# A two-layer encoder: weight low halves moved to VectorE, output sums merged over two head groups, Newton steps in two operations

## The chip, the cores and the metric

The kernel runs on one core of a Trainium2 chip. The metric is the device time of one execution in microseconds (us): the median of several runs, beside one execution that was profiled. Engines are named as in the profile: PE is TensorE's matmul, PEld its weight load, DVE is VectorE, ACT is ScalarE, POOL is GpSimd, SP is SyncE, which issues most of the transfers.

## The reference

Input is a token matrix of 512 x 1024 in float32. Layer 0 mixes neighbourhood attention and a bidirectional state-space scan, layer 1 is grouped-query attention; a SwiGLU feed-forward layer follows each. The change works mostly on layer 1:

```python
def odd_mixer(x, mix_norm, w_qkv, q_norm, k_norm, w_out):
    proj = rms_norm(x, mix_norm) @ w_qkv
    q, k, v = jnp.split(proj, [1024, 1280], axis=-1)
    q = rms_norm(q.reshape(Bsz, S, 16, 64), q_norm)   # 16 query heads
    k = rms_norm(k.reshape(Bsz, S, 4, 64), k_norm)    # 4 key heads
    v = v.reshape(Bsz, S, 4, 64)
    q = apply_rope(q, cos, sin)
    k = apply_rope(k, cos, sin)
    return gqa_block_attention(q, k, v) @ w_out       # softmax over 512 keys
...
def rms_norm(x, g):
    return x * lax.rsqrt(jnp.mean(x * x, axis=-1, keepdims=True) + 1e-6) * g
...
    x = x + odd_mixer(...)
    x = x + swiglu_ffn(x, ...)
```

## The kernel before

The residual lies transposed in eight tiles `res[o]` of 128 x 512. Float32 accuracy on TensorE comes from splitting each operand: `hi` is the value rounded to the matmul's format (a copy on ScalarE), `lo` is what is left (a subtraction). `mm3` (L157) then issues three matmuls for a product: low weights by high input, high weights by low input, high by high (L160, L161, L162).

`load_w` (L139) brings a block of weights, 128 x 1024, into `raw` (two buffers), writes the high half on ScalarE (L147) and the low half with the engine given by `eng`, VectorE if none is given (L149). High and low halves have three buffers each. `stream` (L166) walks through a list of blocks, loads two blocks ahead of the one whose matmuls it yields, and yields after each step of three matmuls, so that a caller can take the matmuls piece by piece as filling between other work.

In `odd_mixer` (L1123) the order is this. `prep` (L178) splits the scaled residual, two projections into the banks `kpa` and `kpb` give the keys (`project`, L173), `sumsq` (L774) adds the squares of the residual on GpSimd (L191), and `rotate` and `head_rstd` norm and turn the keys. Query group 0 follows (`q_blocks`, L1223), then the values (L1350 to L1352), whose weights' low halves are made on GpSimd (L1341). Query groups 1 to 3, two blocks of weights each, and the output projection of head groups 0 to 2, two blocks each, are the filling of the attention loop; the low halves of all of these twelve blocks are made on GpSimd. `q_finish` (L1242) runs four steps behind the last matmul of a query group and holds the norm and the rotation, almost all on VectorE.

The attention loop has 35 steps. Step i issues scores for 256 queries of a head (`scores`: two banks, maximum on VectorE L1268, exponent on ScalarE L1270, reciprocal on VectorE L1271, scaling on GpSimd L1272), the transposes of step i - 2 (L1281, split by L1284 and L1285) and the product with the values of step i - 3 (L1298, L1299). Between them it takes so many filling steps as `quota` says:

```python
quota = (5, 5, 4) + 13 * (2,) + (3, 2, 2, 2, 2, 3, 2, 2, 2, 2, 3, 2, 2, 3, 2, 2, 3, 3, 3)
```

When a pair of heads is through, `values` splits its result into `ctxb[h // 2]` (low part on GpSimd up to head 13, L1155). `out_blocks(part)` idles, yielding nothing to do, until both pairs of its head group are there; then it multiplies for each of eight output tiles into a bank of its own and adds the bank to the residual on VectorE (L1320). Banks for this and for the query projections are three in rotation. The last head group goes through `tail` behind the loop.

An inverse square root is a logarithm and an exponent on ScalarE, improved by one Newton step in three VectorE operations: r (1.5 - 0.5 m r r). It stands in `rsqrt_tile` (L205 to L207, tiles of 128 x 512), `rsqrt_small` (L213 to L216, a few columns) and in the feed-forward layer's `norm` (L1042 to L1044).

The order of instructions on an engine is the written one only inside the feed-forward layers and, for TensorE, in the state-space part of layer 0. Elsewhere a planner orders them: in the written order, but what it takes to be ready goes ahead of what is not.

Of the kernel before, what the change touches and what calls it, by code (L numbers as in the profile page):

```python
# [12 lines left out]
ALU = mybir.AluOpType  # L13
# [4 lines left out]
P = 128  # L18
# [23 lines left out]
DT_STEP = 96  # L42
LEAD = (12, 12, 12, 0)
# [29 lines left out]
def encoder_kernel(ctx: ExitStack, tc: tile.TileContext, xt, vec, cst, rope, nab, w_v, w_qk, w_dt, w_ssd,  # L73
# [99 lines left out]
    def project(ps, src, xg, name, eng=None):  # L173
        w = load_w(src, 1024, name, eng)
        for k in range(KB):
            mm3(ps, w, k * P, xg[k], ALL, k == 0, k == KB - 1)
# [21 lines left out]

    def rsqrt_tile(m, name):
        r = slot(f"{name}_r")  # L200
        t = slot(f"{name}_t")
        A.activation(r, m, AF.Ln)
        A.activation(r, r, AF.Exp, scale=-0.5)
        A.activation(t, r, AF.Square)
        V.tensor_tensor(t, t, m, ALU.mult)  # L205
        V.tensor_scalar(t, t, -0.5, 1.5, ALU.mult, ALU.add)
        V.tensor_tensor(r, r, t, ALU.mult)  # L207
        return r

    def rsqrt_small(m, r, t):  # L210
        A.activation(r, m, AF.Ln)
        A.activation(r, r, AF.Exp, scale=-0.5)
        V.tensor_tensor(t, r, r, ALU.mult)  # L213
        V.tensor_tensor(t, t, m, ALU.mult)
        V.tensor_scalar(t, t, -0.5, 1.5, ALU.mult, ALU.add)
        V.tensor_tensor(r, r, t, ALU.mult)  # L216
# [563 lines left out]
    def ffn(layer, gname, hp):  # L780
# [232 lines left out]
        with tc.manual_schedule(engines={mybir.EngineType.PE, mybir.EngineType.DVE, mybir.EngineType.Activation}):  # L1013
# [19 lines left out]
            def norm():  # L1033
                ps = bank(f"{name}_ss", "c")
                T.matmul(ps, ones_r, ql, start=True, stop=False)
                T.matmul(ps, ones_r, qh, start=False, stop=True)
                m, r, t = (slot(f"{name}_{n}") for n in "mrt")
                A.activation(m, ps, AF.Identity, scale=1.0 / D, bias=epst)
                A.activation(r, m, AF.Ln)
                A.activation(r, r, AF.Exp, scale=-0.5)  # L1040
                A.activation(t, r, AF.Square)
                V.tensor_tensor(t, t, m, ALU.mult)  # L1042
                V.tensor_scalar(t, t, -0.5, 1.5, ALU.mult, ALU.add)
                V.tensor_tensor(r, r, t, ALU.mult)  # L1044
                rstd.append(r)
# [77 lines left out]
    def odd_mixer(op):  # L1123
# [40 lines left out]
        project(pa, w_kv[0], xg, "wka")  # L1164
        project(pb, w_kv[1], xg, "wkb")
        acc = sumsq("o")
# [56 lines left out]
        def q_blocks(g, eng):  # L1223
            banks = []

            def matmuls(w):
# [7 lines left out]
                if len(sqs) == 2:  # L1234
                    V.tensor_tensor(sqs[0], sqs[0], sqs[1], ALU.add)
                    after(4, lambda: q_finish(g, banks, sqs[0]))
# [74 lines left out]
        def out_blocks(part):  # L1311
            def matmuls(w, half):
                while ctxb[2 * part + 1] is None:
                    yield
                for o in range(4 * half, 4 * half + 4):
                    ps = bank(f"o1{part}_{o}")
                    for k in range(2):
                        mm3(ps, w, (o % 4 * 2 + k) * P, ctxb[2 * part + k], ALL, k == 0, k == 1)
                        yield
                    V.tensor_tensor(res[o], res[o], ps, ALU.add)  # L1320

            for half in range(2):
                yield (lambda half=half: load_w(w_o1[part, half], 1024, f"wo{part}_{half}", G)), \
                    (lambda w, half=half: matmuls(w, half))
# [9 lines left out]
        for c in range(4):  # L1334
# [6 lines left out]
            G.tensor_tensor(lo, part, f(hi), ALU.subtract)  # L1341
            wv.append((hi, lo))
        vhl = []
        for t in range(4):
            ps = bank(f"gv{t}", "s")
            for k in range(KB):
# [15 lines left out]
        blocks = (list(q_blocks(1, G)) + list(q_blocks(2, G)) + list(q_blocks(3, G))  # L1362
                  + [b for part in range(3) for b in out_blocks(part)])
        fill = stream(blocks, 2)
        run(fill, 8)
# [3 lines left out]
        quota = (5, 5, 4) + 13 * (2,) + (3, 2, 2, 2, 2, 3, 2, 2, 2, 2, 3, 2, 2, 3, 2, 2, 3, 3, 3)  # L1369
        lag_t, lag_v = 2, 3  # L1370
        for i in range(32 + lag_v):
            n = quota[i]
# [153 lines left out]
```

## Time and profile before

| | |
|---|---|
| median of 3 timed runs | 1289.76 us (1288.01 to 1290.24) |
| the profiled execution's own time | 1290.49 us |
| its span, first to last instruction | 1288.7 us |
| mean granted TensorE clock | 0.995 |
| busy: PE, DVE, ACT, POOL | 1264.0, 1000.4, 716.1, 166.4 us |
| the mixer of layer 1 in the span | 718 to 937 us |

Busy time is the time in which the engine's records lie; matmuls overlap in these records, so a matmul's duration is longer than its distance to the next. A wait is idle time of an engine, put down to what released it.

### The profile page before, as it was taken

How to read it: one execution, taken by the hardware profiler on the slowest of the kernel's cores; microseconds unless marked ns; L12 is line 12 of the kernel's file. 1: busy time of each engine (PE TensorE's matmuls, PEld its weight loads, DVE VectorE, ACT ScalarE, POOL GpSimd, SP SyncE). 2: the span in 40 equal slices, each digit the busy share in tenths (PEclk: the TensorE clock that was granted, in tenths of full speed). 3: DMA queues.
4: the chain of work that ended last, by engine and by line, in shares of the span. 5: the costliest groups of instructions: out<-in, count | busy, mean ns of one | idle time of the engine just before them, and what ended most of it. 6: DMA issues, size and time to landing. Idle time of an engine off the chain costs nothing.

```text
span 1288.7 us, 20006 instructions
## 1 busy us (share of the span) xinstructions
PE 1264.0 (98%) x7502; PEld 1101.0 (85%) x7502; DVE 1000.4 (78%) x1688; ACT 716.1 (56%) x1335; POOL 166.4 (13%) x184
## 2 busy tenths in 40 slices
PE   9999999989999999999999999999999999999998
PEld 8777788867888899989998778778888899889987
DVE  6788798997789898738953668998889998549732
ACT  6676568766455456514643547777565455325521
POOL 5022111011100000000002334655100000000000
PEclk9999999999999999999999999999999999999999
DMA  7334343545333333332223443321223333423132
GB/s 235 107 99 148 112 138 123 164 120 166 123 116 113 99 99 114 117 98 84 91 78 96 144 97 101 83 66 34 83 82 98 106 107 104 123 79 105 54 117 92
DMA packets 52081, 139.03 MB, mean 108 GB/s; under 512 B 6992, under 2 KB 8144, under 8 KB 51984
## 3 DMA queue, kind: packets, MB, share of 16 engines
q1 hardware_dynamic: 51696, 137.23, 34.7%
q8 instruction: 59, 0.97, 0.3%
q10 hardware_dynamic: 288, 0.52, 0.1%
q14 instruction: 38, 0.31, 0.1%
HBM read 127.11 MB, written 2.23 MB: 100 GB/s over the span
## 4 chain that ended last, share of the span: by engine, by line
PE 70%; DVE 17%; ACT 6%; issue 4%; DMA 2%; SPq 0%; POOL 0%; ACTq 0%; DVEq 0%; POOLq 0%
PE fo L160 5%; PE fo L162 5%; PE fo L161 5%; PE fa L162 5%; PE fa L161 5%; PE fa L160 5%; PE fb L161 3%; PE fb L160 3%; PE fb L162 3%; PE vps L278 2%; PE opt L1281 1%; PE fc L162 1%; PE fc L161 1%; PE fc L160 1%; PE fg L1009 1%
## 5 line engine op out<-in xcount | busy, mean ns | idle before, releaser
L147 ACT ACTIVATE wf_h<-wf_r 128x1024 fp32r<-128x1024 f32 (+1 forms) x76 | 69.5, 919 | 125.8 <-PE fo L162 68.3
L160 PE MATMUL fo<-hh,wf_l 128*128 128x512 f32 x352 | 137.2, 390 | 1.2 <-DVE wf_l L149 1.2
L161 PE MATMUL fo<-hl,wf_h 128*128 128x512 f32 x352 | 137.0, 389 | 0.0
L162 PE MATMUL fo<-hh,wf_h 128*128 128x512 f32 x352 | 136.9, 389 | 0.0
L984 DVE TENSOR_TENSOR xr<-xr,fo 128x512 f32<-128x512 f32 x48 | 32.2, 685 | 113.6 <-PE fo L162 113.6
L149 DVE TENSOR_TENSOR wf_l<-wf_r,wf_h 128x1024 fp32r<-128x1024 f32 (+1 forms) x76 | 78.8, 1053 | 15.0 <-ACT wf_h L147 15.0
L160 PEld LDWEIGHTS fo<-hh,wf_l 128*128 128x128 f32 x352 | 66.1, 188 | 15.5 <-DVE wf_l L149 2.0
L162 PEld LDWEIGHTS fo<-hh,wf_h 128*128 128x128 f32 x352 | 66.1, 188 | 13.8
L161 PEld LDWEIGHTS fo<-hl,wf_h 128*128 128x128 f32 x352 | 66.1, 188 | 13.6
L160 PE MATMUL g<-n_xh,w_l 128*128 128x512 f32 x192 | 76.6, 399 | 0.0
L162 PE MATMUL g<-n_xh,w_h 128*128 128x512 f32 x192 | 75.3, 392 | 0.0
L161 PE MATMUL g<-n_xl,w_h 128*128 128x512 f32 x192 | 75.2, 392 | 0.0
L910 ACT ACTIVATE sl<-sb 128x256 f32<-128x256 f32 x34 | 14.3, 419 | 90.7 <-DVE sb L909 90.7
L191 POOL TENSOR_TENSOR o_acc<-o_acc,o_sq 128x512 f32<-128x512 f32 x7 | 12.3, 1753 | 383.2 <-ACT o_sq L190 383.2
L1272 POOL TENSOR_SCALAR op<-op,osum 128x512 f32<-128x512 f32 x64 | 45.4, 718 | 55.5 <-DVE osum L1271 38.6
L1270 ACT ACTIVATE op<-os,omx 128x512 f32<-128x512 f32 x64 | 43.6, 686 | 15.1 <-DVE omx L1268 12.9
L1285 DVE TENSOR_TENSOR opt<-opt,opt 128x512 fp32r<-128x512 f32 x64 | 43.5, 683 | 7.2 <-ACT opt L1284 6.5
L1284 ACT ACTIVATE opt<-opt 128x512 fp32r<-128x512 f32 x64 | 37.9, 598 | 18.7 <-PE opt L1281 18.1
L791 ACT ACTIVATE sa<-fa 128x256 f32<-128x256 f32 x68 | 25.4, 374 | 36.3 <-PE fa L162 36.3
L1268 DVE TENSOR_REDUCE omx<-os 128x1 f32<-128x512 f32 x64 | 42.0, 679 | 4.5 <-PE os L1266 4.4
L791 ACT ACTIVATE gh<-gr 128x1024 fp32r<-128x1024 f32 x34 | 35.6, 1047 | 14.0 <-PE fo L162 11.6
L162 PEld LDWEIGHTS g<-n_xh,w_h 128*128 128x128 f32 x192 | 36.1, 188 | 7.5
(2644 smaller groups left out, 4363.9 us busy)
## 6 DMA issues: line engine op xcount, KB each, us to landing
ur<-in_w_fa SPq DMA_DIRECT2D x34, 512.0 KB, 3.6
gr<-in_w_fa SPq DMA_DIRECT2D x34, 512.0 KB, 3.5
w_r<-in_w_ssd SPq DMA_DIRECT2D x24, 512.0 KB, 3.7
wf_r<-in_w_fa SPq DMA_DIRECT2D x20, 512.0 KB, 3.6
wf_r<-in_w_fb SPq DMA_DIRECT2D x32, 320.0 KB, 3.0
wf_r<-in_w_fb SPq DMA_DIRECT2D x16, 512.0 KB, 3.5
wo_r<-in_w_o SPq DMA_DIRECT2D x14, 512.0 KB, 3.8
nb<-in_nab SPq DMA_DIRECT2D x16, 256.0 KB, 3.0
```

Of the source, the lines that this page charges most:

```text
L147: A.activation(hi[:, 0:cols], raw, AF.Copy)
L149: (eng or V).tensor_tensor(lo[:, 0:cols], raw, f(hi)[:, 0:cols], ALU.subtract)
L160: T.matmul(ps, wl[:, a], xh[:, b], start=first, stop=False, skip_group_check=skip)
L161: T.matmul(ps, wh[:, a], xl[:, b], start=False, stop=False, skip_group_check=skip)
L162: T.matmul(ps, wh[:, a], xh[:, b], start=False, stop=last, skip_group_check=skip)
L791: A.activation(dst, src, AF.Copy, scale=scale)
L984: V.tensor_tensor(res[o], res[o], self.banks[o], ALU.add)
L1268: V.tensor_reduce(mx, sps, AX.X, ALU.max, negate=True)
L1270: A.activation(p_, sps, AF.Exp, bias=mx, accum_out=sums)
L1272: G.tensor_scalar(p_, p_, sums, 1.0, ALU.mult, ALU.mult)
L1284: A.activation(hl[:, 0:S], pt, AF.Copy)
L1285: V.tensor_tensor(hl[:, S:2 * S], pt, f(hl[:, 0:S]), ALU.subtract)
```

## The change

- `project` loses its `eng` and gains `late`: for the first key projection the eight matmuls with the low part of the input come last. `sumsq("o")` runs on VectorE.
- The low halves of the value weights, of query groups 1 to 3 and of the output blocks are made on VectorE.
- `out_blocks` takes a list of head groups. Groups 0 and 1 form one list: each output tile is summed over both in one bank and added to the residual once, in four blocks of two output tiles; group 2 keeps two blocks of four. A block of the merged list is loaded in two transfers of 512 columns.
- The Newton step is one function of two operations, each with a scalar and two tensors.
- The numbers of filling steps, the four steps of delay and the eight steps before the loop get names; their values stay.

```diff
--- before.py
+++ after.py
@@ -40,6 +40,9 @@
 NSLOT = 12
 NA_QUOTA = (12, 12, 10, 10, 8, 8, 6, 6, 6, 6)
 DT_STEP = 96
+OD_FILL = 8
+OD_AFTER = 4
+OD_QUOTA = (5, 5, 4, 2, 2, 2, 2, 2, 2, 2, 2, 2, 2, 2, 2, 2, 3, 2, 2, 2, 2, 3, 2, 2, 2, 2, 3, 2, 2, 3, 2, 2, 3, 3, 3)
 LEAD = (12, 12, 12, 0)
 SSD_QUOTA = ((10, 8, 10, 2, 12), (10, 8, 10, 2, 12), (10, 8, 10, 2, 12), (10, 8, 10, 2, 12))
 NORM_LAG = (12, 12, 6, 14)
@@ -170,10 +173,13 @@
                 ws.append(blocks[len(ws)][0]())
             yield from matmuls(ws[n])
 
-    def project(ps, src, xg, name, eng=None):
-        w = load_w(src, 1024, name, eng)
-        for k in range(KB):
-            mm3(ps, w, k * P, xg[k], ALL, k == 0, k == KB - 1)
+    def project(ps, src, xg, name, late=False):
+        wh, wl = load_w(src, 1024, name)
+        order = [(k, p) for k in range(KB) for p in range(3)]
+        if late:
+            order = [(k, p) for k in range(KB) for p in (0, 2)] + [(k, 1) for k in range(KB)]
+        for m, (k, p) in enumerate(order):
+            T.matmul(ps, (wl if p == 0 else wh)[:, k * P:k * P + P], xg[k][p == 1], start=m == 0, stop=m == 23)
 
     def prep(xt, g, name, mk=xgslot):
         hi, lo = mk(f"{name}_xh"), mk(f"{name}_xl")
@@ -196,24 +202,24 @@
         A.activation(m, ps, AF.Identity, scale=inv, bias=epst)
         return rsqrt_tile(m, name)
 
+    def newton(r, t, m):
+        V.scalar_tensor_tensor(t, t, -0.5, m, ALU.mult, ALU.mult)
+        V.scalar_tensor_tensor(r, t, 1.5, r, ALU.add, ALU.mult)
+
     def rsqrt_tile(m, name):
         r = slot(f"{name}_r")
         t = slot(f"{name}_t")
         A.activation(r, m, AF.Ln)
         A.activation(r, r, AF.Exp, scale=-0.5)
         A.activation(t, r, AF.Square)
-        V.tensor_tensor(t, t, m, ALU.mult)
-        V.tensor_scalar(t, t, -0.5, 1.5, ALU.mult, ALU.add)
-        V.tensor_tensor(r, r, t, ALU.mult)
+        newton(r, t, m)
         return r
 
     def rsqrt_small(m, r, t):
         A.activation(r, m, AF.Ln)
         A.activation(r, r, AF.Exp, scale=-0.5)
         V.tensor_tensor(t, r, r, ALU.mult)
-        V.tensor_tensor(t, t, m, ALU.mult)
-        V.tensor_scalar(t, t, -0.5, 1.5, ALU.mult, ALU.add)
-        V.tensor_tensor(r, r, t, ALU.mult)
+        newton(r, t, m)
 
     def bcast_rstd(acc, name):
         ps = bank(f"{name}_ss", "c")
@@ -1039,9 +1045,7 @@
                 A.activation(r, m, AF.Ln)
                 A.activation(r, r, AF.Exp, scale=-0.5)
                 A.activation(t, r, AF.Square)
-                V.tensor_tensor(t, t, m, ALU.mult)
-                V.tensor_scalar(t, t, -0.5, 1.5, ALU.mult, ALU.add)
-                V.tensor_tensor(r, r, t, ALU.mult)
+                newton(r, t, m)
                 rstd.append(r)
 
             def tick(i, n, ps):
@@ -1161,9 +1165,9 @@
 
         ktab = rope_tabs("gq_k", "kt")
         pa, pb = bank("kpa"), bank("kpb")
-        project(pa, w_kv[0], xg, "wka")
+        project(pa, w_kv[0], xg, "wka", True)
         project(pb, w_kv[1], xg, "wkb")
-        acc = sumsq("o")
+        acc = sumsq("o", V)
         ksq = [slot(f"oksq{n}") for n in range(2)]
         for n, ps in enumerate((pa, pb)):
             A.activation(ksq[n], ps, AF.Square)
@@ -1233,7 +1237,7 @@
                 sqs.append(sq)
                 if len(sqs) == 2:
                     V.tensor_tensor(sqs[0], sqs[0], sqs[1], ALU.add)
-                    after(4, lambda: q_finish(g, banks, sqs[0]))
+                    after(OD_AFTER, lambda: q_finish(g, banks, sqs[0]))
 
             sqs = []
             for n in range(2):
@@ -1308,20 +1312,29 @@
             if j % 2 == 1:
                 ctxb[h // 2] = split(cx, f"cx{h}", xgslot if h >= 12 else ctxslot, V if h >= 14 else G)
 
-        def out_blocks(part):
-            def matmuls(w, half):
-                while ctxb[2 * part + 1] is None:
+        def out_blocks(parts):
+            per = 8 // (2 * len(parts))
+
+            def matmuls(w, t):
+                while ctxb[2 * parts[-1] + 1] is None:
                     yield
-                for o in range(4 * half, 4 * half + 4):
-                    ps = bank(f"o1{part}_{o}")
-                    for k in range(2):
-                        mm3(ps, w, (o % 4 * 2 + k) * P, ctxb[2 * part + k], ALL, k == 0, k == 1)
-                        yield
+                for n in range(per):
+                    o = per * t + n
+                    ps = bank(f"o1{parts[0]}_{o}")
+                    for m, part in enumerate(parts):
+                        for k in range(2):
+                            mm3(ps, w, ((m * per + n) * 2 + k) * P, ctxb[2 * part + k], ALL, m + k == 0,
+                                k == 1 and part == parts[-1])
+                            yield
                     V.tensor_tensor(res[o], res[o], ps, ALU.add)
 
-            for half in range(2):
-                yield (lambda half=half: load_w(w_o1[part, half], 1024, f"wo{part}_{half}", G)), \
-                    (lambda w, half=half: matmuls(w, half))
+            def load(t):
+                half, at = divmod(t * per, 4)
+                return load_w([w_o1[part, half][:, 2 * P * at:2 * P * (at + per)] for part in parts], 1024,
+                              f"wo{parts[0]}_{t}", V)
+
+            for t in range(8 // per):
+                yield (lambda t=t: load(t)), (lambda w, t=t: matmuls(w, t))
 
         def run(gen, n=None):
             for _ in (gen if n is None else range(n)):
@@ -1338,7 +1351,7 @@
                 nc.sync.dma_start(raw, w_gv[c // 2])
             part = raw[:, c % 2 * S:(c % 2 + 1) * S]
             A.activation(hi, part, AF.Copy)
-            G.tensor_tensor(lo, part, f(hi), ALU.subtract)
+            V.tensor_tensor(lo, part, f(hi), ALU.subtract)
             wv.append((hi, lo))
         vhl = []
         for t in range(4):
@@ -1359,17 +1372,16 @@
             V.tensor_tensor(vh[:, :, 1], v4, f(vh[:, :, 0]), ALU.subtract)
             vhl.append(v)
             step(True)
-        blocks = (list(q_blocks(1, G)) + list(q_blocks(2, G)) + list(q_blocks(3, G))
-                  + [b for part in range(3) for b in out_blocks(part)])
+        blocks = (list(q_blocks(1, V)) + list(q_blocks(2, V)) + list(q_blocks(3, V))
+                  + [b for parts in ((0, 1), (2,)) for b in out_blocks(parts)])
         fill = stream(blocks, 2)
-        run(fill, 8)
+        run(fill, OD_FILL)
         step(True)
         for j in range(1, GQ_KV):
             stack_k(j)
-        quota = (5, 5, 4) + 13 * (2,) + (3, 2, 2, 2, 2, 3, 2, 2, 2, 2, 3, 2, 2, 3, 2, 2, 3, 3, 3)
         lag_t, lag_v = 2, 3
         for i in range(32 + lag_v):
-            n = quota[i]
+            n = OD_QUOTA[i]
             cuts = (0, (n + 2) // 3, (2 * n + 2) // 3, n)
             if i < 32:
                 scores(i)
```

## Rows read from the trace of the kernel before

**Rows 1.** The page's busy time, share of the span and instructions of each engine.
```profile
PE 1264.0 (98%) x7502; PEld 1101.0 (85%) x7502; DVE 1000.4 (78%) x1688; ACT 716.1 (56%) x1335; POOL 166.4 (13%) x184
```

**Rows 2.** Stretches: length, busy (count) PE, PEld, DVE, ACT, POOL, clock, DMA.
```profile
743.00:754.00 11.00, 8.75 (x58) 7.12 (x57) 10.96 (x18) 4.21 (x8) 2.83 (x2) 1.00 0.52 129
803.00:824.00 21.00, 18.73 (x103) 14.31 (x102) 20.61 (x34) 16.60 (x35) 15.42 (x12) 1.00 0.26 80
838.00:862.00 24.00, 21.55 (x116) 17.71 (x115) 23.86 (x44) 17.71 (x36) 15.18 (x14) 0.93 0.20 58
862.00:937.00 75.00, 74.83 (x440) 64.05 (x439) 63.42 (x120) 49.32 (x101) 25.95 (x31) 1.00 0.20 63
```

**Rows 3.** Waits of TensorE, 700 to 960 us: total us, times, longest.
```profile
PE oc L1298 <- DVE opt L1285: 1.7, 1, 1.7
...
PE oq_ss L1185 <- DVE oqsq L1235: 1.3, 1, 1.3
...
PE gv L1350 <- DVE oq_m L1187: 0.7, 1, 0.7
...
PE kpa L161 <- DVE o_xl L181: 0.5, 1, 0.5
```

**Rows 4.** The same view, 838 to 862 us.
```profile
PE os L1265 <- ACT op L1270: 1.5, 1, 1.5
PE opt L1281 <- DVE opt L1285: 0.9, 1, 0.9
```

**Rows 5.** VectorE's timeline: start us, us, line, operation, tiles, shapes, count.
```profile
721.23 2.44 DVE L181 SCALAR_TENSOR_TENSOR o_xl<-xr,vect,o_xh 128x512 fp32r<-128x512 f32 x2
...
735.03 2.33 DVE L213 TENSOR_TENSOR ortt<-ort 128x4 f32<-128x4 f32 x1
...
742.18 1.80 DVE L205 TENSOR_TENSOR ok_t<-ok_t,ok_m 128x512 f32<-128x512 f32 x1 [2.10 <-ACT ok_t L204]
...
807.34 2.07 DVE L1145 TENSOR_TENSOR q_ra<-q_ra,q_rb 128x512 f32<-128x512 f32 x1
...
817.84 3.50 DVE L1247 TENSOR_TENSOR q_ra<-q_ra,oq_r 128x512 f32<-128x512 f32 x2
...
851.79 2.66 DVE L207 TENSOR_TENSOR oq_r<-oq_r,oq_t 128x512 f32<-128x512 f32 x1
```

**Rows 6.** Groups by line and shape, whole span: busy us, mean ns, idle before.
```profile
L1272 POOL TENSOR_SCALAR op<-op,osum 128x512 f32<-128x512 f32 x64 | 45.4, 718 | 55.5 <-DVE osum L1271 38.6 <-PE opt L1281 11.0 <-PE oc L1299 4.3
...
L1320 DVE TENSOR_TENSOR xr<-xr,o 128x512 f32<-128x512 f32 x24 | 16.2, 674 | 0.9 <-PE o L162 0.7
...
L149 DVE TENSOR_TENSOR wq_l<-wq_r,wq_h 128x1024 fp32r<-128x1024 f32 x6 | 7.3, 1220 | 2.5 <-ACT wq_h L147 2.5
...
L821 DVE SCALAR_TENSOR_TENSOR xa<-xr,vect,fr_r 128x512 f32<-128x512 f32 x8 | 5.9, 741 | 0.0
...
L206 DVE TENSOR_SCALAR gn_t<-gn_t 128x512 f32<-128x512 f32 x4 | 3.4, 847 | 0.0
...
L206 DVE TENSOR_SCALAR kn_t<-kn_t 128x512 f32<-128x512 f32 x4 | 1.7, 419 | 0.0
```

**Rows 7.** GpSimd's timeline, columns as in rows 5.
```profile
720.72 1.73 POOL L191 TENSOR_TENSOR o_acc<-o_acc,o_sq 128x512 f32<-128x512 f32 x1 [5.57 <-ACT o_sq L190]
...
734.52 2.82 POOL L149 TENSOR_TENSOR wq_l<-wq_r,wq_h 128x1024 fp32r<-128x1024 f32 x1
```

**Rows 8.** The chain that ended last, 936 to 950 us: start us, us, what.
```profile
943.50 5.44 PE fu L1009 x24
```

**Rows 9.** GpSimd's groups, 803 to 824 us.
```profile
L149 POOL TENSOR_TENSOR wo_l<-wo_r,wo_h 128x1024 fp32r<-128x1024 f32 x2 | 5.3, 2670 | 0.3 <-ACT wo_h L147 0.3
...
L149 POOL TENSOR_TENSOR wq_l<-wq_r,wq_h 128x1024 fp32r<-128x1024 f32 x1 | 2.4, 2373 | 0.8 <-ACT wq_h L147 0.8
```

**Rows 10.** Instructions on the banks o, 838 to 856 us (PE, PEld, DVE).
```profile
838.00:856.00 18.00, 8.38 (x30) 5.34 (x30) 1.36 (x2) 1.00 0.15 44
```

**Rows 11.** Waits of TensorE, first 400 us.
```profile
PE oA L160 <- ACT cf L636: 4.6, 1, 4.6
```

## The prediction

> **What bounds the kernel now.** I read the page's busy shares first: TensorE is busy for 98% of the span [rows 1], so the change can give back only what TensorE loses, and I looked for the places where it loses. The table of stretches over the grouped-query mixer shows three: between 743 and 754 us TensorE works 8.75 of 11 us, between 803 and 824 us 18.73 of 21, between 838 and 862 us 21.55 of 24, there with a granted clock of 0.93 [rows 2]. In the same three VectorE works 10.96, 20.61 and 23.86 us: it is full. From 862 to 937 us it is the other way round: TensorE 74.83 of 75, VectorE 63.42 [rows 2]. The waits of TensorE in the mixer name VectorE, with one exception [rows 3, 4]; that one, on ScalarE, lies in the last of the three stretches, where ScalarE's exponent waits for VectorE's maxima.
>
> Why is VectorE late? Its timeline has operations that take far too long: a product of 4 columns takes 2.33 us, a product of 512 columns 1.80 or 2.66, a sum 2.07, two products together 3.50 [rows 5], where an addition of 512 columns usually takes 0.67 [rows 6]. GpSimd's timeline at those moments shows why: it is writing a low half. The 2.33 us operation starts at 735.03 and ends at 737.36; GpSimd's low half starts at 734.52, takes 2.82 and ends at 737.34. The same holds at 721: two low parts of the input take 2.44 us, and GpSimd's last sum of squares ends at 722.45 [rows 5, 7]. So a VectorE operation that reads two SBUF tiles stands still until GpSimd's one is through. That is the first fact of this case: GpSimd's 16 low halves cost VectorE time at the moments when VectorE holds TensorE up.
>
> **The change part by part.** *First key projection and sum of squares.* TensorE waits 0.5 us in the first key bank for the last low part [rows 3]. The new order puts the eight products with that part last, 16 products of 0.227 us (5.44 us for 24 [rows 8]) later than the first, and the sum of squares, now on VectorE, can't block it. I take -0.5. The seven sums cost VectorE 0.67 each by the nearest row [rows 6] in a stretch before 720 where the down projection keeps TensorE busy; uncovered they could cost 0.7 (the last one) and no more.
>
> *Low halves on VectorE.* Twelve of 1024 columns move: 2.4 to 2.8 us each on GpSimd [rows 7, 9], 1.22 on VectorE [rows 6]; four of 512 columns for the values, by the nearest row about 0.67. VectorE gets 12 x 1.22 + 4 x 0.67 = 17.3 us more work over some 200 us, and its long blocks go. What that is worth I read stretch by stretch.
>
> 743 to 754: TensorE loses 2.25 us [rows 2], in waits of 1.3 and 0.7 and small ones [rows 3]. The chain in front of them holds a block of at least 2.33 - 0.67 = 1.7 us and one of 1.80 - 0.67 = 1.1 [rows 5]. Into the same chain come two low halves of the values and one of a query weight, 2.6 us; the next one fits while VectorE waits for ScalarE's square root. The two-operation Newton step gives 0.42 - 2 x 0.07 = 0.28 back (below). So the chain gets some 0.5 us shorter up to the root and 1.4 more behind it, where the sum of squares for the query norm and the copies that free the banks stand in the queue. Of 2.25 us lost I take 1.6 back; bounds 0 and 2.25.
>
> 803 to 824: the norm of query group 2. The blocks give back 2.07 - 0.67 = 1.4 and 3.50 - 2 x 0.67 = 2.2 us, the Newton step 0.28; three low halves fall into this stretch [rows 9], 3 x 1.22 = 3.66. The balance is -0.2. Loads may come to lie in calmer places, as the planner orders VectorE by readiness, so I take -0.5 of the 2.27 us that are lost; bounds +1.2 (one more low half) and -2.3.
>
> 838 to 862: the norm of group 3. The block of 2.66 us falls to 0.74 (-1.9), the Newton step gives 0.28, one low half comes in (+1.22; the later ones wait for buffers), and three of the output sums leave (below), -2.0. VectorE: -3.0.
>
> *Merged output sums.* Eight of 24 additions into the residual go, 0.67 us each [rows 6], 5.4 us of VectorE. TensorE's matmuls stay the same in number. But the order changes: a bank now needs head pairs 0 to 3, where the first group alone needed pairs 0 and 1. Before, TensorE ran 30 output matmuls between 838 and 856 us [rows 10], as filling while softmax was late. Now the generator idles until pair 3 is there, seven steps of the quota (3 + 2 + 2 for i = 16 to 18), and pair 3 comes only at the end of i = 18. That is 30 x 0.227 = 6.8 us of work that leaves this stretch and comes later. The planner can bring forward what is ready: of each bank the half that belongs to pairs 0 and 1, two steps of three matmuls, in the three banks of the rotation: 18 matmuls. Then 12 x 0.227 = 2.7 us are missing. TensorE's loss there would be 2.45 + 2.7 - 3.0 = 2.1 us, a gain of 0.3; bounds +6.8 (nothing brought forward, VectorE's relief without effect) and -2.45. The granted clock of 0.93 over 24 us is 1.7 us more of loss there; its two waits, 1.5 and 0.9 us [rows 4], are what TensorE does there besides working. If the waits shrink a little it can stay up or not: I take half, -0.8. Behind 862 us the late matmuls fill TensorE as before, and ten steps in place of three lie behind the loop, where they need no softmax; VectorE has 11.6 us free there [rows 2] for three more low halves (3.7).
>
> *Newton in two operations.* Removed is the scalar operation, 0.42 us mean, but 0.85 in the four of the group norms [rows 6], where GpSimd's own products can block it; the two products (0.67) become three-operand ones (0.74 [rows 6]). So 0.28 per step, 0.7 in the group norms. Two of the group norms and four key norms lie before 281 us, where TensorE waits 4.6 us for ScalarE's decay, which stands in a chain with VectorE's work [rows 11]: 2 x 0.7 + 4 x 0.28 = 2.5 us of relief at most. How much of it is on the chain I don't see; I take 0.7, bounds 0 and 2.5. The steps in the feed-forward layers are worth nothing: no wait of TensorE hangs on them; if that cover is gone they give 0.28 each.
>
> *What stands in VectorE's queue.* On GpSimd a low half could wait for its high half at no cost. In VectorE's queue the maxima and reciprocals of softmax stand behind it, and TensorE's next transposes behind these. The nearest row has six low halves with 2.5 us of such waits [rows 6], 0.4 each; five fall into the three stretches (one, three, one), so 2.0 us at worst, which are part of the upper bounds. The four more transfers are hidden: a block is asked for two blocks ahead, 16 steps of 3 x 0.227 = 11 us.
>
> In the rows VectorE stands still for GpSimd's whole operation [rows 5, 7]; without such meetings the sum below is -4.4, with one for each of those five low halves it is -0.8 (second rival). The Trainium skill, page "SBUF — State Buffer", section "Who interferes with whom", has the rule to it: a VectorE instruction with two SBUF inputs and a GpSimd instruction that reads SBUF lock each other out, and whoever comes second waits for the whole of the other. The trace agrees (2.33 us for 4 columns). By the rule a low half on VectorE, with its two SBUF inputs, can be locked out as well, which speaks against this change.
>
> **Sum.** -0.5 (key projection) -1.6 -0.5 -0.3 -0.8 (clock) -0.7 = -4.4 us. Against the profiled execution's own 1290.49 us this is 1286.1; the median of the timed runs is 0.7 lower, so I predict 1285.4.
>
> **Rivals.** *The hole in the filling makes it slower.* If nothing is brought forward, 6.8 us of TensorE's work leave 838 to 856 us, and the clock falls once more as in rows 2 (1.7): +8.5. Against it stand -0.5 - 1.6 - 0.5 - 0.7, so +5.2: 1295. It decides from the point where the hole costs more than 3.3 + 2.6 us. For it: the stretch is VectorE's, and the query groups' matmuls are used up by then. Against it: TensorE did 30 output matmuls there where the quota asks for 21, so the planner does bring work forward. Chance 0.20.
>
> *GpSimd still blocks.* 64 scalings of 0.72 us [rows 6] and 13 low parts stay on GpSimd. If each of the five low halves in the three stretches waits for one such scaling, that is 5 x 0.72 = 3.6 us, and the balance is -0.8: 1289, within the noise. For it: the scalings come at the pace of softmax, two per step. Against it: the scaling reads a single tile, and its blocks in the rows of before were short. Chance 0.24, with all other ways to break even.
>
> *All of the losses go.* 0.5 + 2.25 + 2.3 + 2.4 + 1.7 + 2.5 = 11.6 us: 1278. The low halves would have to fall into VectorE's gaps everywhere. Chance 0.06. The forecast itself has 0.50.
>
> A change of under 0.2% (2.6 us) can hardly be told from none. Faster by more: 0.56; within: 0.24; slower: 0.20. The range, 1278.5 to 1293: below, it takes in nearly all of the losses; above, most of the rival of the hole, of which the worst part (1 in 10) stays out. The forecast's own range is 1281 to 1287.
>
> **What would show it.** Right: no wait in the first key bank; no VectorE operation of 4 or 512 columns over 1.5 us after 718; GpSimd's busy time down by over 29 us (12 x 2.4 and the values and sums); TensorE's loss between the query norms and 862 us down by 3 us or more; the same matmuls in number. Wrong: output matmuls missing where the norm of group 3 runs, with TensorE idle there for 6 us or more; low halves on VectorE of 1.7 us and over; or a loss in the first 300 us that grows, since the planner orders that stage anew as well.

## The result and the profile after

The changed kernel takes 1280.88 us (median of 6 runs, 1279.83 to 1282.27), the kernel before, on the same chip, 1289.36 (1288.01 to 1291.39). The ratio is 0.9933, 95% interval 0.992 to 0.9946: 8.5 us faster, where the prediction had 4.4. The time lies inside the stated range, just below its "own range" of 1281 to 1287.

The page's first line after (busy us, share, instructions):

```profile
PE 1259.5 (98%) x7502; PEld 1097.9 (86%) x7502; DVE 997.0 (78%) x1681; ACT 715.4 (56%) x1335; POOL 123.9 (10%) x161
```

The count of matmuls is that of [rows 1]; GpSimd is busy for 42.5 us less. VectorE is not busier, though it took over 16 low halves and seven sums.

Stretches of the mixer after, columns as in [rows 2]: the norms of query groups 0, 2 and 3, and the rest of the loop.

```profile
737.00:748.00 11.00, 11.00 (x69) 9.49 (x68) 11.00 (x19) 5.02 (x8) 0.00 (x0) 1.00 0.66 171
797.00:818.00 21.00, 20.98 (x117) 17.08 (x116) 20.29 (x36) 16.89 (x35) 9.95 (x11) 1.00 0.27 86
828.00:852.00 24.00, 21.83 (x124) 17.16 (x124) 22.66 (x46) 18.80 (x42) 12.03 (x14) 1.00 0.05 14
852.00:930.00 78.00, 77.19 (x444) 65.23 (x445) 65.39 (x119) 51.30 (x105) 23.05 (x30) 1.00 0.24 72
```

TensorE is full in the first two, where it lost 2.25 and 2.27 us. In the third it still loses 2.2, but the clock stays at 1.00 where it was 0.93.

Not all of this is gain. Over the whole loop, before and after:

```profile
764.80:937.90 173.10, 168.06 (x958) 141.17 (x957) 151.52 (x285) 123.48 (x257) 83.91 (x86) 0.99 0.28 78
```

```profile
759.00:930.00 171.00, 167.12 (x954) 138.92 (x953) 150.75 (x283) 122.25 (x256) 64.35 (x77) 1.00 0.28 78
```

TensorE is idle for 5.0 us before and 3.9 after: about half of what the second stretch gave back is lost again at other places of the loop.

Waits of TensorE after, from the first feed-forward layer to the end (total us, times, longest):

```profile
PE os L1269 <- ACT op L1274: 1.2, 4, 0.5
PE o L164 <- POOL cx_sl L1159: 0.9, 1, 0.9
PE opt L1285 <- DVE opt L1289: 0.7, 1, 0.7
PE oc L1302 <- DVE ocx L1311: 0.6, 1, 0.6
PE fo L163 <- DVE wf_l L152: 0.2, 1, 0.2
```

The waits for the key bank, for the sum of squares and for the norm [rows 3] are gone. A new one, 0.9 us, is that for the low part of a head pair: the merged sums wait for pair 3, as the prediction said. No VectorE operation behind 718 us, low halves included, takes over 1.3 us.

VectorE after, by tile (ns min/median/max), the operations that stood still in [rows 5]:

```profile
L221 DVE TENSOR_TENSOR ortt<-ort x1: 162/162/162, 731.9 to 731.9; 128x4 f32<-128x4 f32 x1
...
L1149 DVE TENSOR_TENSOR q_ra<-q_ra,q_rb x8: 673/680/893, 746.1 to 840.1; 128x512 f32<-128x512 f32 x8
L1251 DVE TENSOR_TENSOR q_ra<-q_ra,oq_r x8: 678/688/1104, 751.5 to 845.8; 128x512 f32<-128x512 f32 x8
```

The product of 4 columns takes 0.16 us in place of 2.33; the longest of the others is 1.1 us, in place of 2.9.

All kernels of this study in one table. Gains in microseconds are by the ratio, 0.001 being 1.3 us, unless two times stand beside them. The stages are the distances between first matmuls in each trace: the first gate projection of layer 0 (from the span's start), the first key projection, the first scores, the first gate projection of layer 1, the end. "Low" is where the granted clock fell to 0.5, the last microseconds of the span left out. Such a stretch lasts 3.4 us, the one at 285 us mostly 6.8; at half clock 3.4 us cost 1.7 at most, an estimate (before, output matmuls follow each other at 0.43 us in the stretch at 858 us, at 0.23 us at 848).

| kernel | ratio to before (95%) | layer 0 | FFN 0 | keys, values | loop | FFN 1 | low, us |
|---|---|---|---|---|---|---|---|
| before | | 371.2 | 346.8 | 46.8 | 173.1 | 350.8 | 80, 285, 858 |
| changed | 0.9933 (0.992 to 0.9946) | 368.9 | 346.4 | 43.7 | 171.0 | 350.3 | 284 |
| e1 Newton alone | 0.9964 (0.9951 to 0.9976) | 367.9 | 346.4 | 46.5 | 172.5 | 350.4 | 283, 853 |
| e2 low halves alone | 0.9979 (0.9966 to 0.9992) | 369.4 | 346.8 | 45.1 | 171.7 | 351.0 | 80, 284 |
| e3 merge alone | 0.9991 (0.9981 to 1.0) | 372.5 | 346.8 | 47.6 | 171.9 | 350.7 | 81, 286, 750 |
| e4 key part alone | 1.0 (0.9988 to 1.0012) | 371.6 | 346.9 | 46.7 | 173.1 | 350.8 | 80, 285, 749, 858 |
| e5 changed, no merge | 0.9926 (0.9914 to 0.9939) | 366.7 | 346.4 | 43.8 | 170.3 | 350.3 | 281 |
| e6 changed, old Newton | 0.9975 (0.9964 to 0.9985) | 369.2 | 346.8 | 44.2 | 172.6 | 350.7 | 284 |
| e7 before, low halves cut | 0.9962 (0.9949 to 0.9975) | 371.9 | 346.8 | 46.6 | 168.5 | 350.9 | 81, 285 |
| e8 changed, all on VectorE | 0.9962 (0.9949 to 0.9976) | 368.0 | 346.4 | 43.8 | 175.1 | 350.3 | 283, 853 |
| e9 combined | 0.9898 (0.9885 to 0.9912) | 367.7 | 346.4 | 42.6 | 168.7 | 350.4 | 285 |
| e10 combined, more cut | 0.9904 (0.989 to 0.9918) | 368.4 | 346.4 | 42.8 | 168.7 | 350.4 | 283 |
| e11 combined, layer 0 cut | 0.9894 (0.9879 to 0.9909) | 366.3 | 346.4 | 42.7 | 168.7 | 350.8 | 283 |
| e12 Newton in part | 0.9968 (0.9957 to 0.9979) | 368.9 | 346.9 | 47.1 | 173.2 | 350.8 | 283, 747, 856 |

So the 8.4 us by which the span shrank lie: 2.3 in layer 0, 0.4 and 0.5 in the feed-forward layers, 3.1 ahead of the loop, 2.1 in it. In layer 0 one execution tells little: before, e2, e3, e4, e6 and e7 run the same instructions there in the same order, and take 369.2 to 372.5 us. Together the profiles tell more: the eight kernels with the short Newton step there take 366.3 to 368.9 us, all less than these six, and the means are 3.1 us apart.

The clock differs between executions of one kernel, too. Of the 53 executions of the kernel before that were timed beside e1 to e12, the 17 with a mean clock of 0.993 take 1291.3 us on average, the six with 0.997 take 1288.2. That is 3.1 us where the clock lost by 0.004 amounts to 5.2, so, as an estimate, a low stretch goes with about 1 us and not with all of its 1.7. The four executions of the changed kernel with 0.997 take 1281.3 on average: at an equal mean clock it is 6.9 us faster, and by this estimate some 1.6 of the 8.5 us go with the clock.

### The profile page after: what moved, and what is told of

Same layout as the page of the kernel before. It is cut to its first block, busy times and chain, and to the rows that moved or that the text cites. A ratio compares the mean times of both kernels' runs of the same rounds, so it can differ in the third digit from the quotient of the medians.

```text
span 1280.3 us, 19973 instructions
## 1 busy us (share of the span) xinstructions
PE 1259.5 (98%) x7502; PEld 1097.9 (86%) x7502; DVE 997.0 (78%) x1681; ACT 715.4 (56%) x1335; POOL 123.9 (10%) x161
## 4 chain that ended last, share of the span: by engine, by line
PE 74%; DVE 14%; ACT 6%; issue 3%; DMA 2%; POOL 0%; SPq 0%; ACTq 0%; DVEq 0%; POOLq 0%
PE fo L163 5%; PE fo L165 5%; PE fo L164 5%; PE fa L165 5%; PE fa L164 5%; PE fa L163 5%; PE fb L165 3%; PE fb L164 3%; PE fb L163 3%; PE opt L1285 2%; PE vps L284 2%; PE fc L165 1%; PE fc L164 1%; PE fc L163 1%; PE fg L1015 1%
## 5 line engine op out<-in xcount | busy, mean ns | idle before, releaser
L1276 POOL TENSOR_SCALAR op<-op,osum 128x512 f32<-128x512 f32 x64 | 48.0, 756 | 507.9 <-DVE osum L1275 492.2
L164 PEld LDWEIGHTS g<-n_xl,w_h 128*128 128x128 f32 x192 | 36.1, 188 | 7.4 <-DVE n_xl L187 0.8
```

The source lines that it names most:

```text
L164: T.matmul(ps, wh[:, a], xl[:, b], start=False, stop=False, skip_group_check=skip)
L1276: G.tensor_scalar(p_, p_, sums, 1.0, ALU.mult, ALU.mult)
```

## The experiments

**Each part alone: e1 to e4.** The theory was that the low halves carry the gain and the Newton step more than the prediction gave it; the rivals, that the planner's new order or the fewer additions do it.

e1, all Newton steps:

```diff
-        V.tensor_tensor(t, t, m, ALU.mult)
-        V.tensor_scalar(t, t, -0.5, 1.5, ALU.mult, ALU.add)
-        V.tensor_tensor(r, r, t, ALU.mult)
+        V.scalar_tensor_tensor(t, t, -0.5, m, ALU.mult, ALU.mult)
+        V.scalar_tensor_tensor(r, t, 1.5, r, ALU.add, ALU.mult)
```

> The kernel before with the Newton steps in two operations and nothing else. The change as a whole gave 8.5 us, of which the marks in its trace place 2.3 in the first mixer, 0.4 and 0.5 in the feed-forward layers. If the shorter Newton step is what helps there: 2.5 to 4 us faster than before, with the first feed-forward layer starting about 2 us earlier. Rival, as the prediction had it (0.7): not more than 1 us, and the 2.3 us come from the planner's new order alone.

1285.95 us against 1290.64, 4.6 us faster: more than expected. Waits of TensorE in the first 400 us (the warm-up left out):

```profile
PE oA L160 <- ACT cf L636: 4.6, 1, 4.6
PE yd L650 <- DVE cf L645: 2.3, 2, 1.3
PE kss L359 <- ACT ksq L357: 1.4, 1, 1.4
```

The wait of [rows 11] stands as it was. What is gone is a wait of 1.9 us for the low half of key weights at 78 us, and with it the low clock at 80; a wait of 1.4 came.

e2, the low halves:

```diff
-        blocks = (list(q_blocks(1, G)) + list(q_blocks(2, G)) + list(q_blocks(3, G))
+        blocks = (list(q_blocks(1, V)) + list(q_blocks(2, V)) + list(q_blocks(3, V))
...
-                yield (lambda half=half: load_w(w_o1[part, half], 1024, f"wo{part}_{half}", G)), \
+                yield (lambda half=half: load_w(w_o1[part, half], 1024, f"wo{part}_{half}", V)), \
...
-            G.tensor_tensor(lo, part, f(hi), ALU.subtract)
+            V.tensor_tensor(lo, part, f(hi), ALU.subtract)
```

> The kernel before with the 16 low halves (query groups 1 to 3, output blocks, value weights) on VectorE and nothing else. If GpSimd's two-tensor operations block VectorE, their removal gives 3 to 5 us in the mixer of layer 1, though VectorE gets 17 us more work. Rival: VectorE is full in the loop, so without the eight additions that the merge takes away it is no faster, or slower by up to 2 us.

2.7 us faster by the ratio (0.21% of 1290), just short of the expected 3 to 5. VectorE's low halves for the output, in groups by shape (busy us, mean ns):

```profile
L149 DVE TENSOR_TENSOR wo_l<-wo_r,wo_h 128x1024 fp32r<-128x1024 f32 x14 | 17.9, 1281 | 4.7 <-ACT wo_h L147 4.7
```

Eight of the 14 are those of layer 0. The mean is 0.06 us over the 1.22 of [rows 6]: 0.9 us in all, put down to waits for GpSimd, as layer 0's eight have 1.22 in this trace and the other six 1.36.

e3, the merge, with GpSimd still making the low halves:

```diff
+            for t in range(8 // per):
+                yield (lambda t=t: load(t)), (lambda w, t=t: matmuls(w, t))
...
-                  + [b for part in range(3) for b in out_blocks(part)])
+                  + [b for parts in ((0, 1), (2,)) for b in out_blocks(parts)])
```

> The kernel before with the output sums of head groups 0 and 1 merged, low halves still on GpSimd. If the filling that is missing while the norm of group 3 runs costs time: 1 to 4 us slower than before. Rival: eight additions less on a full VectorE: 1 to 3 us faster.

0.9991, with an interval that reaches 1.0: a loss of 1 us or more is excluded, a gain is not shown. The loop is 1.2 us shorter, without the low clock at 858, but one came at 750.

e4, the late order and `sumsq("o", V)`:

> The kernel before with the late order in the first key projection and the sum of squares on VectorE, nothing else. Wait of 0.5 us in the first key bank gone: 0.5 to 0.7 us faster, within what can be told. Rival: the sums on VectorE delay the low parts, and nothing or a loss of up to 1 us comes out.

No difference. The wait in the key bank is gone, but the one behind it grew from 1.3 [rows 3] to 2.0 us, and the clock fell with it. The waits between 700 and 770 us, and the stretch around the low clock:

```profile
PE oq_ss L1188 <- DVE oqsq L1238: 2.0, 1, 2.0
```

```profile
743.00:756.00 13.00, 10.71 (x67) 9.51 (x66) 11.65 (x18) 5.86 (x10) 3.11 (x2) 0.87 0.46 113
```

TensorE came earlier to the same late VectorE. The four parts sum to 4.6 + 2.7 + 1.2 + 0 = 8.5 us, the gain of the whole; with 1.2 to 1.7 us of uncertainty on each, that it fits so closely is luck.

**Two parts undone: e5 and e6.** e5 is the changed kernel with `((0,), (1,), (2,))` in place of `((0, 1), (2,))`.

> The changed kernel with the output sums of groups 0 and 1 separate again, six blocks of which all low halves are on VectorE. If the parts add up, the merge is worth about 1 us: 7 to 8 us faster than the kernel before. If the full VectorE needs the merge to carry the low halves: only 4 to 6 us faster, with waits of TensorE back between 800 and 860 us. If the hole in the filling does cost time: faster than the changed kernel, 9 to 11 us.

1280.91 us, ratio 0.9926, 9.6 us faster than before, beside 0.9933 for the changed kernel: the intervals overlap, the merge is worth nothing that can be told where VectorE makes the low halves. The second answer falls. The time lies where the third one put it, but the difference from the changed kernel is not shown, though the loop is 0.7 us shorter in this one profile.

e6 is the changed kernel with the three-operation step.

> The changed kernel with Newton steps in three operations again. The Newton step alone gave 4.6 us, so 3.5 to 5 us should be left of 8.5, with the low clock level back at 80 us behind a wait for the low half of the key weights. Rival, the gain of the Newton step alone was a lucky order that does not carry over: 6.5 us or more are left.

0.9975: 3.2 us are left, so the step is worth some 5. The wait of 1.9 us for the key weights' low half is back, the low clock behind it is not (1.00 between 76 and 84 us), so that expectation was half right, as far as the profiled execution goes (mean clock 0.997; six of the twelve have 0.995 or 0.996, and where they lost it is not on record).

**The block itself: e7.** GpSimd keeps all its low halves, in smaller operations:

```diff
-            (eng or V).tensor_tensor(lo[:, 0:cols], raw, f(hi)[:, 0:cols], ALU.subtract)
+            step = 256 if eng is G else cols
+            for c in range(0, cols, step):
+                s_ = slice(c, c + step)
+                (eng or V).tensor_tensor(lo[:, s_], raw[:, s_], f(hi)[:, s_], ALU.subtract)
```

The four low halves of the value weights are not made by this helper and stayed whole.

> The kernel before, where each low half of 1024 columns that GpSimd makes is issued as four operations of 256 columns (the same elements on the same engine, the four of the value weights in two). If VectorE waits for the whole of one GpSimd operation, its blocks of 2 us shrink to under 1 us, and 1 to 3 us of the gain appear with not one low half on VectorE. Rival, VectorE is slowed by the elements that GpSimd reads, however they are cut: blocks of the same sum, no gain; a loss if GpSimd gets slower by the cuts.

0.9962, 4.9 us faster, more than expected; the interval overlaps that of e2 a little. GpSimd works longer (0.81 us per quarter, 3.2 per low half), TensorE, VectorE and ScalarE run the same operations in the same order between the key projection and the second feed-forward layer, and the loop falls from 173.1 to 168.5 us. Of these 4.6 us, 2.8 are waits of TensorE (idle for 5.0 us before, for 2.2 here); the low clock at 858 us is gone as well:

```profile
765.30:933.80 168.50, 166.26 (x958) 139.89 (x957) 147.72 (x285) 123.02 (x257) 89.72 (x113) 1.00 0.29 80
```

That TensorE may start on a quarter before the whole low half is there explains nothing: of its waits before, between 700 and 960 us, none is for GpSimd. VectorE and GpSimd where the block of 3.50 us was [rows 5] (start us, us):

```profile
807.79 1.14 DVE L1148 TENSOR_TENSOR q_ra<-q_ra,q_rb 128x512 f32<-128x512 f32 x1
...
817.21 1.87 DVE L1250 TENSOR_TENSOR q_ra<-q_ra,oq_r 128x512 f32<-128x512 f32 x2
```

```profile
817.79 3.27 POOL L152 TENSOR_TENSOR wo_l<-wo_r,wo_h 128x256 fp32r<-128x256 f32 x4 [0.41 <-ACT wo_h L147]
```

VectorE's two products take 1.87 us, 0.5 more than without a wait, while GpSimd's quarters run: they wait for part of one quarter, not for all four. The small Newton step ahead of the key norm shows the other side, by tile (ns):

```profile
L216 DVE TENSOR_TENSOR ortt<-ort x1: 164/164/164, 736.6 to 736.6; 128x4 f32<-128x4 f32 x1
L217 DVE TENSOR_TENSOR ortt<-ortt,ortm x1: 655/655/655, 736.8 to 736.8; 128x4 f32<-128x4 f32 x1
L218 DVE TENSOR_SCALAR ortt<-ortt x1: 667/667/667, 737.5 to 737.5; 128x4 f32<-128x4 f32 x1
L219 DVE TENSOR_TENSOR ort<-ort,ortt x1: 659/659/659, 738.2 to 738.2; 128x4 f32<-128x4 f32 x1
```

Three operations of 4 columns wait for one quarter each: 1.5 us lost, where one block had lost 2.2. So the cut helps a chain of tiny operations less than long ones. The stage ahead of the loop gains nothing (46.6 us); the low halves of the value weights, whole on GpSimd, lie there too.

**Everything on VectorE: e8.** The changed kernel with the last 13 two-tensor operations of the loop moved as well:

```diff
-            eng = G if g else V
+            eng = V
...
-                ctxb[h // 2] = split(cx, f"cx{h}", xgslot if h >= 12 else ctxslot, V if h >= 14 else G)
+                ctxb[h // 2] = split(cx, f"cx{h}", xgslot if h >= 12 else ctxslot, V)
```

> The changed kernel with the last 13 two-tensor operations of the attention loop (low parts of three query groups and seven head pairs) on VectorE too; GpSimd keeps the scalings of one tensor. They take 1.3 us each on GpSimd, 0.68 on VectorE: 13 x 0.68 = 8.8 us more work for VectorE. If the blocks are what counts: 1 to 2 us faster than the changed kernel, and the wait for a head pair's low part (0.9 us) is gone. Rival, VectorE's work now counts: 1 to 4 us slower than the changed kernel.

The rival holds: 0.9962 beside 0.9933, 3.7 us slower than the changed kernel. The loop takes 175.1 us, 4.1 more, of which a low clock at 853 us can be up to 1.7. Its two largest waits, 700 to 960 us:

```profile
PE opt L1285 <- DVE opt L1289: 2.7, 3, 1.6
PE os L1269 <- ACT op L1274: 2.6, 6, 1.2
```

The wait for a head pair's low part is gone, as expected, but 13 operations more on VectorE cost more than their blocks had.

**Put together: e9 to e11.** e9 takes from e5 what helps ahead of the loop and from e7 what helps in it:

```diff
-        blocks = (list(q_blocks(1, V)) + list(q_blocks(2, V)) + list(q_blocks(3, V))
-                  + [b for parts in ((0, 1), (2,)) for b in out_blocks(parts)])
+        blocks = (list(q_blocks(1, V)) + list(q_blocks(2, G)) + list(q_blocks(3, G))
+                  + [b for parts in ((0,), (1,), (2,)) for b in out_blocks(parts)])
```

with the output blocks on GpSimd and the cut of e7.

> The changed kernel without the merge, with the low halves of query groups 2 and 3 and of the output blocks back on GpSimd, but each as four operations of 256 columns; value weights and query group 1 stay on VectorE. By the marks in the traces the stage ahead of the loop should take 43.8 us as with the low halves on VectorE, the loop 168.5 as with the four-part low halves on GpSimd (171.0 in the changed kernel): 1.5 to 3 us faster than the changed kernel, 10 to 11.5 faster than the kernel before. Rival, the order that the planner finds decides more than the blocks: anywhere within 3 us of the changed kernel.

1277.69 us against 1290.7, ratio 0.9898: 13 us faster than the kernel before and 4.5 faster than the changed one, more than expected. The loop is as added up (168.7 us), the stage ahead of it 1.2 us shorter (42.6). This version beats both kernels; its interval meets neither that of the changed kernel nor that of e5. From e5 it differs only in the low halves of the loop, cut on GpSimd in place of whole on VectorE: 3.6 us. Waits of TensorE in its mixer:

```profile
PE os L1272 <- ACT op L1277: 1.0, 1, 1.0
PE opt L1288 <- DVE ocx L1314: 1.0, 1, 1.0
PE opt L1288 <- POOL op L1279: 0.3, 1, 0.3
```

e10 cuts the 13 low parts of the loop into two operations each.

> The run before it, with the 13 low parts of query groups and head pairs on GpSimd cut into two operations of 256 columns as well. Blocks of up to 1.3 us become 0.7: up to 0.5 us faster than that run. Rival: GpSimd's fixed cost for 13 more operations delays the head pair's low part for which the output matmuls wait: 0.5 us slower.

0.9904, the same loop: no difference, on either side.

e11 cuts the 16 two-tensor operations of layer 0's state-space part on GpSimd into halves of 256 columns.

> The combined kernel with the 16 two-tensor operations of the state-space part in layer 0 (1.4 us each on GpSimd) cut into halves. If the block lasts as long as GpSimd's single operation there too, VectorE's stretched operations in layer 0 lose about half of their 7 us, and the output projection of that layer starts 0.5 to 2 us earlier. Rival: VectorE's chain there waits for something else (decay rows, ScalarE), and nothing changes.

0.9894 beside 0.9898: the times don't tell them apart. TensorE's waits for the decay in the scan are 1.6 us in place of 2.4, but that of 4.6 us ahead of the output projection is there as before. Layer 0's output projection starts at 282.8 us, e9's at 284.7, and layer 0 is 1.4 us shorter; with runs of one order 3.3 us apart in that stage, this stays open.

**Where the Newton step works: e12.** The kernel before with the short step in the first mixer's input and key norms and the small ones only.

> The kernel before with two-operation Newton steps only in the first mixer's input norm, key norms and the small ones; group norms, query norms and feed-forward norms keep three. If the gain of the Newton step hangs on the wait for the key weights' low half and the low clock level behind it, which end near 83 us: 2 to 3 us of the 4.6. If it is spread over all norms: 1 us.

0.9968, 4.1 us, as much as all steps together within the intervals; the profile of this run has the low clock at 747 and 856 us and shows a smaller gain, 1.8 us of span. By the stages layer 0 has what e1 has to within its spread, the feed-forward layers and the stages of layer 1 have nothing. All but one of the steps that are shortened here lie before 105 us, so most of the gain hangs on these; the intervals leave room for 2 us of the others.

## Why the prediction was right

The direction, the blocks and, roughly, the size of what the mixer of layer 1 gives hold: the sum had 3.7 us for it, its two stages lost 5.2. The rest of the difference between 4.4 and 8.5 us is the Newton step, and that the time still fell into the range is due to the width of the range.

**Blocks by GpSimd: right.** The reading of [rows 5] and [rows 7] is shown by e7: with equal orders on the other engines, cutting GpSimd's operations alone gives 4.9 us. At an equal mean clock of 0.996 it is still 4.4 (1285.2 us, mean of e7's five executions, against 1289.6, of seven of the kernel before), so the clock is the smaller part of it. By the Trainium skill, page "SBUF — State Buffer", section "Who interferes with whom", whoever comes second waits for one whole instruction of the other. The trace of e7 agrees: between quarters of 0.74 us VectorE's operations of 4 columns take 0.66.

**Stretches: right in sum, in part by luck.** Ahead of the loop the sum had -0.5 and -1.6, the stage lost 3.1 us; the two loop stretches and the clock had -1.6, the loop lost 2.1. TensorE's waits in the loop fell by 1.2 us, and the clock at 858 us, which the sum had at half its 1.7, is the rest in this profile. The single terms fit less well. The second stretch gave back all of its 2.25 us where 0.5 were taken, but half of that is lost again at other places of the loop. In the third VectorE's busy time fell by 1.2 us, not by 3.0. (TensorE's waits for ScalarE in the mixer were two, not one: 0.2 us for a value bank as well.)

**Key projection: right in the trace, worth nothing alone.** The wait of 0.5 us goes, but VectorE's next result comes no earlier (e4).

**Merged sums: the hole is there and costs little.** Output matmuls on the banks after, in the 18 us that answer to [rows 10], as the norm of group 3 starts 10 us earlier:

```profile
828.00:846.00 18.00, 4.98 (x18) 3.35 (x19) 0.00 (x0) 1.00 0.02 6
```

Eighteen, where 30 ran in [rows 10]: 12 are missing, as predicted. But the planner brings forward 27, not 18, before the low part of pair 3 is there, as the parts of pair 2 in the three banks come early too, and six of them run before 828 us. TensorE's loss in the stretch is 2.2 us, near the 2.1 of the prediction; since the relief of VectorE in it was smaller than 3.0, that agreement is luck. The rival of the hole did not come true (e3, e5), and the merge as a whole is not shown to give anything.

**GpSimd locking out the low halves: the price was too high.** 3.6 us in the rival; 0.9 in e2. In the changed kernel the 14 low halves `wo_l` have a mean of 1.22 us, so none, while GpSimd's scalings take 0.76 us in place of 0.72 [rows 6]. In e6 it is the other way round, 1.24 and 0.72; who waits changes from kernel to kernel.

**The Newton step: right that it helps, wrong in size and place.** The sum had -0.7. Alone it gives 4.6 us (e1), and 3.2 of the 8.4 us of the span lie in layer 0 and the feed-forward layers, where nothing else was changed. Three things were off. First, the two products were to become operations of 0.74 us, by a row with a gain per partition; after the change they are as long as the products were in the key norms, `kn` (groups by shape, busy us, mean ns):

```profile
L207 DVE SCALAR_TENSOR_TENSOR gn_r<-gn_t,gn_r 128x512 f32<-128x512 f32 x4 | 3.6, 898 | 0.0
L206 DVE SCALAR_TENSOR_TENSOR gn_t<-gn_t,gn_m 128x512 f32<-128x512 f32 x4 | 3.5, 871 | 3.3 <-ACT gn_t L214 3.2
...
L206 DVE SCALAR_TENSOR_TENSOR kn_t<-kn_t,kn_m 128x512 f32<-128x512 f32 x4 | 2.8, 690 | 3.1 <-ACT kn_t L214 3.1
...
L207 DVE SCALAR_TENSOR_TENSOR kn_r<-kn_t,kn_r 128x512 f32<-128x512 f32 x4 | 2.7, 684 | 0.0
```

so a step gives the whole 0.42, not 0.28. In the group norms, `gn`, both operations are stretched, and a step there gives 0.5 (0.69 + 0.85 + 0.75 before), not 0.7. Second, "the steps in the feed-forward layers are worth nothing: no wait of TensorE hangs on them" was false. Each layer has one such step, and before, each had one wait, of 0.6 us, for a low half of the down projection. It comes 53 us behind the norm, at 443 us, but VectorE is busy for 50.6 of the 55 us between. Of the kernel before, 365 to 700 us:

```profile
PE fo L160 <- DVE wf_l L149: 0.6, 1, 0.6
```

After, 0.15 is left in each, so the wait lost what the step lost, its scalar operation of 0.43 us. In the table all kernels with the short step in those norms have 346.4 in the first feed-forward layer and all others 346.8 or 346.9. Third, the place in layer 0 was wrong: the wait of [rows 11] did not move (4.6 us in e1). The gain lies earlier, at 78 us, in a wait that the prediction did not look at; of the twelve steps before 281 us it counted six, without the input norm and the five of a few columns. The 8 us around it before and after (columns as in [rows 2]; the planner's order is another):

```profile
76.00:84.00 8.00, 5.60 (x22) 3.60 (x21) 6.80 (x18) 5.10 (x14) 1.86 (x4) 0.79 0.54 147
```

```profile
74.00:82.00 8.00, 6.57 (x32) 4.67 (x31) 7.91 (x21) 6.21 (x17) 2.86 (x4) 1.00 0.67 180
```

TensorE waits less and keeps its clock. The clock is the smaller part: at an equal mean clock e1 is 3.5 us faster than the kernel before (1286.1 us, four executions at 0.996, against 1289.6), the changed kernel 4.2 faster than e6 (1281.3 against 1285.5 at 0.997). How the rest divides in layer 0 between the shorter chain and the planner's new order is not settled: no run has the one without the other.

## What to carry to other kernels

Where an engine that sets the pace shows single operations several times their usual length, look at what GpSimd does in the same microseconds: its long two-tensor operations cost VectorE whole, and cutting them into quarters can be worth more than moving them (e9 against e5, 3.6 us). In this kernel it paid to move them ahead of the loop, where VectorE runs a chain of tiny operations, and to cut them in the loop, where its operations are long; moving more cost time (e8). Before an edit to a shared helper is costed at nothing, list TensorE's waits in every stage that calls it, with the clock behind each: a wait of 2 us can cost up to 1.7 us more after it has ended.

## What the runs showed of the hardware

VectorE and GpSimd alternated instruction by instruction in e7: three VectorE operations of 4 columns took 0.66 us each between GpSimd's quarters, a scalar operation with one tensor among them; the one before them, ahead of the quarters, took 0.16.

At some waits of 1.5 to 2.7 us the granted clock fell to 0.5 (1.2 GHz) for 3.4 us, at others of such length it did not (e6 at 80 us, 1.9 us of waiting). Eight of the 14 profiles have such a stretch in the mixer of layer 1 or at 80 us, and one is up to 0.13% of the time.
